# A two-layer hybrid trunk on one core: TensorE in program order through the softmax attention, GLA read-outs of a chunk tile together, and the last gate's products from the last tokens down

## The chip, the core and the metric

The kernel runs on one core of a Trainium2 chip. The metric is the device time of one execution in microseconds; a lower time is better. The engines are named as in the profile: PE is TensorE (PEld its weight loads), DVE is VectorE, ACT is ScalarE, POOL is GpSimd and SP is SyncE, whose queue issues DMAs. Each engine takes its instructions in the order of its own queue and waits on semaphores for the others.

## The reference, cut to what matters

Two layers over 16 meta tokens and 1024 tokens (1040 in all), model width 1024. Each layer projects the normalised input to two head groups: four heads of gated linear attention (GLA), read out from the state at the end of each chunk of 64 tokens and gated by `silu(gr)`, and eight heads of softmax attention with a forgetting bias (FoX). Their normalised outputs go through one output projection; a gated convolutional FFN follows.

```python
def chunk_kv_summary(k, v, log_a):
    log_b = jnp.cumsum(log_a, axis=3)
    log_end = log_b[:, :, :, -1:, :]
    u = jnp.einsum('bhntk,bhntv->bhnkv', k * jnp.exp(log_end - log_b), v)
    return u, jnp.exp(log_end[:, :, :, 0, :])
...
    def step(s, inp):                       # GLA: state at the end of chunk c
        u_c, d_c = inp
        s = d_c[..., None] * s + u_c
        return s, s
    o_r = jnp.einsum('bhntk,bhnkv->bhntv', q_r, states)
...
        logits = (jnp.einsum('bqhd,bkhd->bhqk', q_b, kf)          # FoX
                  + c_b[..., None] - c_k[:, :, None, :])
        logits = jnp.where(key_pos[None, :] <= q_pos[:, None], logits, -jnp.inf)
        return jnp.einsum('bhqk,bkhd->bqhd', jax.nn.softmax(logits, axis=-1), vf)
...
        o_gla = rms_norm(o_gla, gla_norm) * jax.nn.silu(gr)
        h = h + jnp.concatenate([o_gla, rms_norm(o_fox, fox_norm)], axis=-1) @ w_out[i]
        h = h + conv_ffn(rms_norm(h, ffn_norm[i]), w_up[i], conv_w[i], conv_b[i], w_down[i])
```

## The kernel before

**Layout and products.** Activations lie transposed, 128 channels by 1040 tokens a tile. Every dense product is done as three products of split operands (`mm3`, L212 to L218): high times high, low times high, high times low. `unit` (L225) is one tile of 128 output channels over one chunk of tokens, a generator that yields after each of its eight input tiles (seven for the output projection here); `add_tile` (L246) makes one unit for each chunk of tokens. A `Work` list holds such units, and `work.run(us)` issues as many of their steps as fill `us` microseconds by the kernel's own formula; `work.drain()` issues all that is left. So the code itself decides, in its program order, which dense products stand between the pieces of attention.

**Who sets the order on an engine.** The program is written in tiles, and a planner then orders each engine's instructions. It takes them by priority, which is the place in the program, unless a piece is raised with `high_priority(8)` (L800, the scores), and an instruction whose operands the planner does not expect to be ready yet is passed by others. Inside a `manual_schedule` block the named engine keeps program order. The FFN already stands in such a block for PE (L1350); GLA and FoX do not.

**GLA** (`gla_steps`, L474, two passes per layer with two heads each). For each tile group of tokens (16, 384, 384 and 256 of them) PE transposes the keys, `fill(0.5)`; PE makes the increments `u` of all its chunks (L500), `fill(1.0)`; then chunk by chunk DVE makes the next state `St` (L508, from four buffers), PE reads it out for two heads (L513) and `fill(0.3)` follows. Then ACT and DVE normalise the read-outs, `fill(3.0)`, PE transposes them, ACT scales them to `og` and POOL's queue writes them to memory (`ogd`). `fill` issues products of the next head group, the first pass `gla_products` of the second, the second pass `fox_products` of the first FoX head pair.

**FoX** (`fox`, L752). Four head pairs p, two heads e, nine query tiles i (the first of 112 tokens, the others of 116), in groups (7,8), (5,6), (3,4), (1,2), (0), from the last tokens down. One query tile of one head is a slot n; there are 72 slots and 8 more that run out. What a tile needs after its scores is put into later slots: transposes T0, T1, T2 of its probabilities at n+2, the P·V products av0, av1, av2 of its group at n+3, the fold of both heads at n+4, and the store at n+6. A slot issues:

```python
            for kind in ('av0', 'T0'):
                run(n, kind)
...
            parts = [c for c in "12" if (n, "av" + c) in due or (n, "T" + c) in due]
            work.run(fill_us / (1 + len(parts)))
            run(n, "store")
            run(n, "fold")
            for c in parts:
                run(n, "av" + c)
                run(n, "T" + c)
                work.run(fill_us / (1 + len(parts)))
```

with the scores of slot n between the first loop and `parts`. A score tile S is made by two products (L649, L650) in one of three PSUM buffers; DVE adds the bias and takes the running minimum in one pass (L652), ACT takes the exponential to P (L664), which frees S. The transposes of P (L678, L685) go to one of two PSUM buffers `tr`, from which ACT copies the high part (L330) and DVE subtracts the low part (L331) into `PT`. The P·V products (L703) and the fold's transposes `fo` (L716) share one PSUM buffer `av`; ACT and DVE empty the fold (L719, L720). The store's transposes (L742) and the V transposes (L583) use `tr` too.

**What fills FoX.** `plan(-1)` is empty and holds for slots 0 to 3. `plan(0)`, `plan(1)` and `plan(2)` start at slots 4, 22 and 40: three products of the next FoX head pair and one gate (`gr_products`, L601). `plan(3)` at slot 58 is the last gate, h = 3, alone; its result goes to `land[3]` in SBUF (`dst`), while the other gates go through memory. A gate unit's `ev` loads `ogd` on SP's queue (L606) and takes five DVE operations after the first reading of PSUM and three on ACT (L609 to L620). `plan(4)` at slot 62 is the output projection of four tiles of channels, from the last tokens down (chunks of 256, 384 and 400 tokens), input tiles in the order `KORD` = 4, 5, 0, 1, 2, 3, 6. Its operands are split by `split(2)`, `split(1)`, `split(0)` (L944), one for each chunk, the first ahead of everything. Weights are loaded one tile ahead on SP's queue, their high parts made by ACT (L183), their low parts in this stage by POOL (L185).

Of the kernel before, what the change touches and what calls it, by code (L numbers as in the profile page):

```python
# [10 lines left out]
F32 = mybir.dt.float32  # L11
# [13 lines left out]
KD = D // 128  # L25
# [10 lines left out]
CH_FOX = [(0, 344), (344, 348), (692, 348)]  # L36
# [4 lines left out]
M_GK, M_GQ, M_GV, M_GR, M_REM, M_FQ, M_FK, M_FV, M_WO, M_UP = 0, 2, 4, 8, 12, 13, 17, 21, 25, 33  # L41
# [91 lines left out]
class Kern:  # L133
# [213 lines left out]
    def head(self, tiles, pp, nm, feed):  # L347
        s = self.slots
        held, w, waiting = [], [], []
        tags = ("mm", "mm", "S", "S", "S")  # L350
        i = 0
# [97 lines left out]
    def gla_decay(self, lyr, p, gp, pp, g):  # L449
# [4 lines left out]
        for c0, n in CH:  # L454
            z = pp.tile([128, 512], F32, tag="S", name="z")
            nc.tensor.matmul(z[:, :n], self.wau[:, lyr, 128 * p:128 * p + 128], rem[0:16, c0:c0 + n],
# [17 lines left out]
    def gla_steps(self, lyr, p, gp, pp, g, fill):  # L474
        nc = self.nc
        gk, gq, gv, gvm, dec = g["gk"], g["gq"], g["gv"], g["gvm"], g["dec"]
        S = None
        tail = []
        for (c0, n), (t0, t1) in zip([(0, META), (META, 384)] + CH[1:], [(0, 1), (1, 4)] + CTILES[1:]):
            nt = t1 - t0  # L480
            rows = META if t0 == 0 else 128
            kd = gp.tile([128, 3, 128], F32, tag="kd", name="kd", bufs=2)
            tr = pp.tile([128, 4, 128], F32, tag="tr", name="tr")
            for j in range(nt):
                nc.tensor.transpose(tr[:rows, j, :], gk[:, c0 + 128 * j:c0 + 128 * j + rows], self.ident[:])
            nc.vector.tensor_copy(kd[:rows, :nt, :], tr[:rows, :nt, :])
            fill(0.5)
            chunks = [(0, 0, META, None)] if t0 == 0 else \
                [(j, 64 * b, 64 * b + 64, 2 * (t0 - 1 + j) + b) for j in range(nt) for b in range(2)]
            o = [pp.tile([128, 4, 128], F32, tag=("av", "tr")[hh], name="o") for hh in range(2)]  # L490
            us = []
            ub = {}
            for j, r0, r1, c in chunks:
                if r0 not in ub:
                    ub[r0] = pp.tile([128, 4, 128], F32, tag="S", name="u")
                u = ub[r0][:, j, :]
                us.append(u)
                for hh in range(2):
                    val = gvm[:, hh, :] if t0 == 0 else gv[hh][r0:r1, t0 - 1 + j, :]
                    nc.tensor.matmul(u[64 * hh:64 * hh + 64, :], kd[r0:r1, j, 64 * hh:64 * hh + 64], val,  # L500
                                     start=True, stop=True)
            fill(1.0)
            for u, (j, r0, r1, c) in zip(us, chunks):
                Sn = gp.tile([128, 128], F32, tag="St", name="St", bufs=4)
                if c is None:
                    nc.vector.tensor_copy(Sn[:], u)
                else:
                    nc.vector.scalar_tensor_tensor(out=Sn[:], in0=S[:], scalar=dec[:, c:c + 1],  # L508
                                                   in1=u, op0=ALU.mult, op1=ALU.add)
                S = Sn  # L510
                q0 = c0 + 128 * j + r0
                for hh in range(2):
                    nc.tensor.matmul(o[hh][r0:r1, j, :], gq[64 * hh:64 * hh + 64, q0:q0 + r1 - r0],  # L513
                                     S[64 * hh:64 * hh + 64, :], start=True, stop=True)
                fill(0.3)
            ons = []
            for hh in range(2):
                ps = o[hh][:rows, :nt, :]
                sq = gp.tile([128, 3, 128], F32, tag="osq", name="osq")
                nc.scalar.activation(sq[:rows, :nt, :], ps, AF.Square)  # L520
                vv = gp.tile([128, 3], F32, tag="ovv", name="ovv", bufs=2)
                nc.vector.tensor_reduce(out=vv[:rows, :nt], in_=sq[:rows, :nt, :], axis=AX.X, op=ALU.add)
                nc.vector.tensor_scalar(out=vv[:rows, :nt], in0=vv[:rows, :nt], scalar1=1.0 / 128,
                                        scalar2=EPS, op0=ALU.mult, op1=ALU.add)
                y0 = gp.tile([128, 3], F32, tag="oy", name="oy", bufs=2)[:rows, :nt]
                a = gp.tile([128, 3], F32, tag="oa", name="oa", bufs=2)[:rows, :nt]
                self.rsqrt(y0, vv[:rows, :nt], y0, a)
                on = gp.tile([128, 3, 128], F32, tag="on", name="on", bufs=2)
                nc.vector.tensor_tensor(out=on[:rows, :nt, :], in0=ps,
                                        in1=y0.unsqueeze(2).to_broadcast([rows, nt, 128]), op=ALU.mult)  # L530
                ons.append(on)
            fill(3.0)
            for hh in range(2):
                tr = pp.tile([128, 4, 128], F32, tag="tr", name="tr")
                for j in range(nt):
                    nc.tensor.transpose(tr[:, j, :rows], ons[hh][:rows, j, :], self.ident[:rows, :rows])
                og = gp.tile([128, 384], F32, tag="og", name="og", bufs=2)
                nc.scalar.mul(og[:, :n], tr[:].rearrange("p a b -> p (a b)")[:, :n],
                              self.v(lyr, V_GN, 2 * p + hh))
                nc.gpsimd.dma_start(self.ogd[2 * p + hh][:, c0:c0 + n], og[:, :n])  # L540
            fill(0.7)
        self.slots.put(gk, gq, *gv)
# [58 lines left out]
    def gr_products(self, lyr, h, work, ap, pp, nm, dst=None):  # L601
        nc = self.nc

        def ev(ps, c0, n):
            og = ap.tile([128, 348], F32, tag="gog", name="gog", bufs=2)
            nc.sync.dma_start(og[:, :n], self.ogd[h][:, c0:c0 + n])  # L606
            e = ap.tile([128, 348], F32, tag="ge", name="ge", bufs=1)
            x = ap.tile([128, 348], F32, tag="vt", name="gx", bufs=self.vt_bufs)[:, :n]
            nc.vector.tensor_tensor(out=x, in0=ps, in1=nm["r"][:, c0:c0 + n], op=ALU.mult)  # L609
            e, og = e[:, :n], og[:, :n]  # L610
            y = ap.tile([128, 348], F32, tag="gy", name="gy", bufs=1)[:, :n]
            nc.vector.tensor_scalar(out=e, in0=x, scalar1=-87.0, scalar2=None, op0=ALU.max)
            nc.scalar.activation(e, e, AF.Exp, scale=-1.0)
            nc.scalar.activation(y, e, AF.Ln, bias=self.ones[:, 0:1])
            nc.scalar.activation(y, y, AF.Exp, scale=-1.0)
            nc.vector.tensor_tensor(out=og, in0=x, in1=og, op=ALU.mult)
            nc.vector.scalar_tensor_tensor(out=e, in0=e, scalar=1.0, in1=y, op0=ALU.add, op1=ALU.mult)
            nc.vector.scalar_tensor_tensor(out=y, in0=e, scalar=-2.0, in1=y, op0=ALU.add, op1=ALU.mult)
            to = e if dst is None else dst[:, c0:c0 + n]
            nc.vector.scalar_tensor_tensor(out=to, in0=y, scalar=-1.0, in1=og, op0=ALU.mult, op1=ALU.mult)  # L620
            if dst is None:
                nc.gpsimd.dma_start(self.mixd[h][:, c0:c0 + n], e)
        self.add_tile(work, pp, self.wm[lyr, M_GR + h], nm["x"], CH_FOX, ev)


    @staticmethod
# [235 lines left out]
    def attention(self, lyr, nm, hsrc, chunks, feed):  # L862
        tc, nc, s = self.tc, self.nc, self.slots
        with tc.tile_pool(name=f"aps{lyr}", bufs=2, space=PSUM, reuse_waits="tile") as pp2, \
                tc.tile_pool(name=f"aps1{lyr}", bufs=1, space=PSUM, reuse_waits="tile") as pp1, \
                tc.tile_pool(name=f"vm{lyr}", bufs=2, reuse_waits="tile") as self.vmp:
            pp = PsumTags({"mm": (pp2, 2), "S": (pp1, 3), "tr": (pp2, 2), "av": (pp1, 1)})
            qs = [{} for _ in range(4)]
            self.vt_bufs = 3
            with tc.tile_pool(name=f"gla{lyr}", bufs=1, reuse_waits="tile") as gp:  # L870
# [25 lines left out]
                work = Work()  # L896
# [18 lines left out]
            with tc.tile_pool(name=f"att{lyr}", bufs=2, reuse_waits="tile") as ap, \  # L915
                    tc.tile_pool(name=f"lent{lyr}", bufs=1, reuse_waits="tile") as lp:
                s.lent = s.add(lp, 2, f"a{lyr}_")
                box = {}
                KORD = (4, 5, 0, 1, 2, 3, 6)

                def plan(p):
# [33 lines left out]
                            first = {} if m else {"w": ready, "before": {0: lambda: split(1), 1: lambda: split(0)}}  # L955
                            self.add_tile(w, pp, self.wm[lyr, M_WO + m], mix, chunks[::-1], ev, ks=KORD, **first)
                    return w
                self.fox(lyr, ap, pp, qs, plan, lambda: box["mix"][KD - 1])
            for m in range(NSPLIT, KD):
                nc.sync.dma_start(box["hT"][m][:, chunks[0][0]:T], hsrc[m][:, chunks[0][0]:T])  # L960
                s.drop(s.lent)
# [469 lines left out]
```

## Time and profile before

| | us |
|---|---|
| median of 3 runs (lowest, highest) | 2668.52 (2667.55, 2669.83) |
| the profiled execution | 2666.38 |
| its span, first to last instruction | 2664.6 |
| PE busy in the span | 2543.8 (95%) |
| mean granted TensorE clock | 0.988 |

The stages of the first layer, in microseconds from the span's start: GLA with its products up to about 193, FoX to 556 (with four tiles of the output projection), the rest of the output projection and the FFN's start to 700, the FFN after that. The second layer's FoX runs from 1510 to 1877.

In the lines of the profile, `out<-in` names the tile that an instruction writes and those it reads; Lnnn is the line of the kernel. In a view of waits the columns are the total idle time, how often, and the longest. In a timeline they are the start, the duration, the engine and what it does, and in brackets the idle time before and who ended it. PE's matmuls are pipelined: one may start before the last is shown as ended.

### The profile page before, as it was taken

Reading aid. Unit: us, or ns where it says so; the run is one execution under the profiler, and the core shown is the slowest. Engines: PE = TensorE matmul, PEld = TensorE weight load, DVE = VectorE, ACT = ScalarE, POOL = GpSimd, SP = SyncE. Lnnn points to the kernel's source line nnn. Section 1 sums busy time; section 2 is a strip of 40 time slices with the busy share of each in tenths; the row PEclk is TensorE's granted clock in tenths of the full one; section 3 lists DMA queues with packets and bytes.
Section 4 is the critical chain, followed back from the end, with each engine's and each line's share of the span. In section 5 each row is a group of like instructions: output and inputs, shape, how many; then the busy total and the mean of one; then the engine's idle time right before and its main releaser. Section 6 shows DMA issues by size and latency. Waiting matters only on the chain.

```text
span 2664.6 us, 46352 instructions
## 1 busy us (share of the span) xinstructions
PE 2543.8 (95%) x18102; PEld 2408.9 (90%) x18102; DVE 1760.6 (66%) x3484; ACT 1240.2 (47%) x2677; POOL 458.1 (17%) x596
## 2 busy tenths in 40 slices
PE   8999999897999999999999999998979999999997
PEld 7888888897999999999998788888979999998886
DVE  7555666759867777643665566666698777776335
ACT  6336665535545445421443455665455444453112
POOL 4023333333000000000200333333320000000002
PEclk9999999998999999999999999999989999999999
DMA  3132133341222222631312222243412222245212
GB/s 124 57 90 52 55 87 114 115 130 62 96 81 76 84 77 91 216 93 57 105 52 64 70 75 60 69 123 100 146 59 90 77 82 80 72 139 197 66 55 76
DMA packets 114476, 240.72 MB, mean 90 GB/s; under 512 B 14432, under 2 KB 36192, under 8 KB 114256
## 3 DMA queue, kind: packets, MB, share of 16 engines
q1 hardware_dynamic: 96000, 182.27, 22.3%
q0 software_dynamic: 16384, 53.18, 5.4%
q8 instruction: 142, 2.33, 0.4%
q10 hardware_dynamic: 1872, 2.31, 0.2%
q14 instruction: 78, 0.64, 0.1%
HBM read 174.01 MB, written 50.91 MB: 84 GB/s over the span
## 4 chain that ended last, share of the span: by engine, by line
PE 62%; issue 18%; DVE 12%; ACT 4%; DMA 2%; POOL 2%; SPq 0%; DVEq 0%; POOLq 0%; ACTq 0%
PE mm L216 12%; PE mm L218 11%; PE mm L217 11%; PE up L216 5%; PE up L218 5%; PE up L217 5%; PE av L703 2%; PE tr L685 2%; DVE S L652 1%; DVE x L1035 1%; PE wo L217 1%; PE wo L216 1%; PE wo L218 1%; DMA cb<-cd 1%; DVE PT L331 1%
## 5 line engine op out<-in xcount | busy, mean ns | idle before, releaser
L216 PE MATMUL up<-x,hi 128*128 128x260 f32 (+1 forms) x2464 | 700.0, 284 | 22.8 <-DVE hu L1177 20.3
L217 PE MATMUL up<-x,lo 128*128 128x260 f32 (+1 forms) x2464 | 698.1, 283 | 0.0
L218 PE MATMUL up<-x,hi 128*128 128x260 f32 (+1 forms) x2464 | 697.4, 283 | 0.0
L216 PEld LDWEIGHTS up<-x,hi 128*128 128x128 f32 x2464 | 466.6, 189 | 24.3 <-DVE hu L1177 20.7
L217 PEld LDWEIGHTS up<-x,lo 128*128 128x128 f32 x2464 | 466.9, 190 | 0.1
L218 PEld LDWEIGHTS up<-x,hi 128*128 128x128 f32 x2464 | 466.9, 189 | 0.0
L216 PE MATMUL mm<-xh,hi 128*128 128x348 f32 (+4 forms) x1056 | 369.8, 350 | 0.0
L218 PE MATMUL mm<-xl,hi 128*128 128x348 f32 (+4 forms) x1056 | 340.8, 323 | 0.0
L217 PE MATMUL mm<-xh,lo 128*128 128x348 f32 (+4 forms) x1056 | 340.4, 322 | 0.0
L1011 DVE TENSOR_TENSOR lo<-raw,hi 128x512 fp32r<-128x512 f32 x308 | 213.4, 695 | 144.4 <-ACT hi L1010 144.4
L183 ACT CAST hi<-raw 128x512 fp32r<-128x512 f32 (+1 forms) x264 | 142.4, 543 | 339.6 <-PE mm L218 249.2
L217 PE MATMUL mm<-ah,lo 128*128 128x400 f32 (+1 forms) x760 | 266.1, 350 | 1.7 <-DVE lo L185 1.7
L216 PE MATMUL mm<-ah,hi 128*128 128x400 f32 (+1 forms) x760 | 265.6, 349 | 0.0
L218 PE MATMUL mm<-al,hi 128*128 128x400 f32 (+1 forms) x760 | 265.6, 349 | 0.0
L185 DVE TENSOR_TENSOR lo<-raw,hi 128x512 fp32r<-128x512 f32 (+1 forms) x196 | 120.8, 620 | 182.6 <-ACT hi L183 179.1
L1010 ACT CAST hi<-raw 128x512 fp32r<-128x512 f32 x308 | 190.2, 620 | 105.7 <-PE up L218 92.2
L216 PEld LDWEIGHTS mm<-xh,hi 128*128 128x128 f32 x1056 | 200.4, 190 | 14.3 <-issue 13.5
L217 PEld LDWEIGHTS mm<-xh,lo 128*128 128x128 f32 x1056 | 200.7, 190 | 0.5 <-issue 0.3
L218 PEld LDWEIGHTS mm<-xl,hi 128*128 128x128 f32 x1056 | 199.6, 189 | 0.3 <-issue 0.3
L1200 POOL DMA_DIRECT2D actd<-cv x44 | 23.4, 533 | 831.1 <-DVE cv L1199 831.1
L331 DVE TENSOR_TENSOR PT<-tr,PT 116x464 fp32r<-116x464 f32 (+3 forms) x240 | 122.3, 516 | 61.4 <-ACT PT L330 59.7
L664 ACT ACTIVATE P<-S,m 116x460 f32<-116x460 f32 (+2 forms) x224 | 125.0, 562 | 79.9 <-DVE m L652 76.5
(248 smaller groups left out, 5287.0 us busy)
## 6 DMA issues: line engine op xcount, KB each, us to landing
raw<-in_wm_dram SPq DMA_DIRECT2D x328, 256.0 KB, 2.6
raw<-in_wd_dram SPq DMA_DIRECT2D x64, 256.0 KB, 2.6
actd<-cv POOLq DMA_DIRECT2D x22, 520.0 KB, 3.0
st<-actd SPq DMA_DIRECT2D x22, 520.0 KB, 4.5
actd<-cv POOLq DMA_DIRECT2D x22, 512.0 KB, 3.0
st<-actd SPq DMA_DIRECT2D x22, 512.0 KB, 4.1
cb<-cd SPq DMA_DIRECT2D x16, 520.0 KB, 4.4
kA<-kA SPq DMA_DIRECT2D x24, 260.0 KB, 3.9
```

The source lines that it names most:

```text
L183: nc.scalar.copy(hi[:, :n, :], raw[:, :n, :])
L185: eng.tensor_tensor(out=lo[:, :n, :], in0=raw[:, :n, :], in1=hi[:, :n, :].bitcast(F32), op=ALU.subtract)
L216: nc.tensor.matmul(ps, wh, xh[:, c0:c0 + n], start=first, stop=False, skip_group_check=more)
L217: nc.tensor.matmul(ps, wl, xh[:, c0:c0 + n], start=False, stop=False, skip_group_check=more)
L218: nc.tensor.matmul(ps, wh, xl[:, c0:c0 + n], start=False, stop=last, skip_group_check=more)
L331: nc.vector.tensor_tensor(out=lo, in0=src, in1=hi.bitcast(F32), op=ALU.subtract)
L652: nc.vector.tensor_tensor_reduce(out=S[:rows, :n], in0=S[:rows, :n], in1=cb[:rows, c0:k1], scale=1.0, scalar=(BIG if ci == 0 else m[:rows, ...
L664: nc.scalar.activation(P[:rows, :n], S[:rows, :n], AF.Exp, scale=-1.0, bias=m[:rows, nch - 1:nch], accum_out=(den if nch == 1 else d3[:row ...
L685: nc.tensor.transpose(tr[:w, j, :rows], P[:rows, o:o + w], id_)
L703: nc.tensor.matmul(av[:, a:width], w.rearrange("p a b -> p (a b)"), x, start=(t == 0 and i == 0), stop=(t == last and i == 1))
L1010: nc.scalar.copy(hi[:], src[:])
L1011: nc.vector.tensor_tensor(out=lo[:], in0=src[:], in1=hi[:].bitcast(F32), op=ALU.subtract)
```

## The change

Three edits. In `gla_steps` all states of a tile group are made first (eight `St` buffers in place of four), then one fill of 0.3 for each chunk together, and then the read-outs of all its chunks. In `gr_products` the last gate, the one with a `dst`, takes its three chunks of tokens from the last to the first. And `fox` is called inside a `manual_schedule` block for PE, so that PE keeps program order through FoX.

```diff
@@ gla_steps
             fill(1.0)
+            Ss = []
             for u, (j, r0, r1, c) in zip(us, chunks):
-                Sn = gp.tile([128, 128], F32, tag="St", name="St", bufs=4)
+                Sn = gp.tile([128, 128], F32, tag="St", name="St", bufs=8)
                 if c is None:
                     nc.vector.tensor_copy(Sn[:], u)
                 else:
                     nc.vector.scalar_tensor_tensor(out=Sn[:], in0=S[:], scalar=dec[:, c:c + 1],
                                                    in1=u, op0=ALU.mult, op1=ALU.add)
                 S = Sn
+                Ss.append(Sn)
+            fill(0.3 * len(chunks))
+            for Sn, (j, r0, r1, c) in zip(Ss, chunks):
                 q0 = c0 + 128 * j + r0
                 for hh in range(2):
                     nc.tensor.matmul(o[hh][r0:r1, j, :], gq[64 * hh:64 * hh + 64, q0:q0 + r1 - r0],
-                                     S[64 * hh:64 * hh + 64, :], start=True, stop=True)
-                fill(0.3)
+                                     Sn[64 * hh:64 * hh + 64, :], start=True, stop=True)
@@ gr_products
-        self.add_tile(work, pp, self.wm[lyr, M_GR + h], nm["x"], CH_FOX, ev)
+        self.add_tile(work, pp, self.wm[lyr, M_GR + h], nm["x"], CH_FOX if dst is None else CH_FOX[::-1], ev)
@@ attention
-                self.fox(lyr, ap, pp, qs, plan, lambda: box["mix"][KD - 1])
+                with tc.manual_schedule(engines={mybir.EngineType.PE}):
+                    self.fox(lyr, ap, pp, qs, plan, lambda: box["mix"][KD - 1])
```

## The prediction

> **What bounds the kernel now.** I read busy time by stage first (per stretch: PE, weight loads, VectorE, ScalarE, GpSimd, then granted clock, DMA share, GB/s), then TensorE's (PE's) waits inside the stages that change, and last the timeline where those waits are.
>
> ```profile
> span 2664.6 us, 46352 instructions
> ...
> 0.00:193.00 193.00, 180.94 (x1225) 155.48 (x1225) 121.18 (x271) 87.68 (x205) 47.07 (x62) 0.99 0.27 88
> 193.00:556.00 363.00, 334.95 (x2310) 316.22 (x2309) 239.81 (x743) 216.43 (x647) 122.73 (x175) 0.99 0.29 85
> ...
> 1510.00:1877.00 367.00, 337.94 (x2312) 319.27 (x2312) 240.24 (x744) 216.40 (x647) 122.69 (x175) 0.98 0.28 84
> ```
>
> PE is the bound: VectorE (DVE) is busy 240 us of a FoX stretch, PE 335 of 363. It idles 28.1 and 29.1 us in the two stretches, and these 57 us, with what half clock costs there, are all that a better order can win. Who ended the idle times (first stretch, then second):
>
> ```profile
> PE tr L685 <- DVE PT L331: 9.4, 9, 2.1
> PE av L703 <- DVE ff L720: 5.2, 8, 1.2
> PE tr L678 <- DVE PT L331: 4.8, 4, 1.9
> PE mm L216 <- ACT mh L330: 4.4, 1, 4.4
> PE mm L217 <- POOL lo L185: 2.0, 3, 1.0
> PE tr L742 <- DVE PT L331: 1.4, 3, 0.7
> ...
> PE tr L685 <- DVE PT L331: 8.5, 9, 1.2
> PE tr L678 <- DVE PT L331: 6.8, 4, 3.5
> PE av L703 <- DVE ff L720: 5.1, 8, 1.2
> PE mm L216 <- ACT mh L330: 4.4, 1, 4.4
> ```
>
> Transposes wait for a PSUM buffer that DVE still reads, 32.3 us in all (9.4+4.8+1.4+8.5+6.8+1.4); the first P·V product after a fold waits for the fold's PSUM bank, 10.3 us; and the output projection waits 4.4 us per layer for one operand.
>
> **Part 1, program order in FoX: the start (+16 us).** The slots n of `fox` take filling products only from slot 4 on: `plan(-1)` is empty. Today the planner lays products of `plan(0)` between the first scores. In program order PE runs scores, transposes and one P·V alone, and all of it hangs on DVE's score pass and ScalarE's (ACT's) exponentials through three S buffers. The timeline shows that chain as it runs today:
>
> ```profile
> 194.46 0.49 PE L583 MATMUL tr<-ident,vt 128*116 128x128 f32 x3
> 196.63 0.64 DVE L652 CUSTOM_DVE_ANT_0 S<-S,cb 116x460 f32<-116x460 f32 x1
> 198.60 0.65 ACT L664 ACTIVATE P<-S,m 116x460 f32<-116x460 f32 x1 [1.64 <-DVE m L652]
> 199.68 0.37 PE L649 MATMUL S<-kA,qA 128*116 128x460 f32 x1
> 201.03 0.86 PE L685 MATMUL tr<-ident,P 116*116 116x116 f32 x7
> 208.64 0.64 ACT L664 ACTIVATE P<-S,m 116x460 f32<-116x460 f32 x1 [0.76 <-DVE m L652]
> 209.09 1.05 PE L703 MATMUL av<-PT,V 112*128 112x232 f32 x7 [0.22 <-DVE PT L331]
> 210.01 0.40 PE L649 MATMUL S<-kA,qA 128*116 128x348 f32 x1
> ...
> 194.95:209.50 14.55, 14.24 (x90) 12.63 (x89) 9.98 (x33) 9.46 (x30) 4.11 (x7) 1.00 0.17 59
> ```
>
> The exponentials of slot 3 begin at 208.64; they free the buffer of slot 4's second score tile, which runs at 210.01. Without products in front it could run some 0.6 us earlier, so filling starts at about 209.5. From 194.95 (the last V transpose) that is 14.5 us. PE's own work in it: nine pairs of score products, at most 0.42 us a pair (3.4; one takes 0.37, a part of which overlaps the next), 21 transposes at 0.09 (1.9; seven start within 0.63), eight P·V at 0.13 (1.0): 6.3 us. So 8.2 us idle against 0.3 now (last row: 14.24 of 14.55): +8 per layer. Bounds: +5, if DVE takes the first scores 2 us earlier and the chain shortens by one; +13, if PE also runs at half clock there.
>
> That clock is seen in the second layer: granted clock by windows (the column before the last two):
>
> ```profile
> 1611.42:1614.40 2.98, 0.99 (x6) 0.98 (x7) 2.12 (x6) 2.65 (x9) 0.00 (x0) 1.00 0.00 0
> 1614.40:1617.80 3.40, 3.40 (x15) 3.27 (x14) 2.36 (x7) 1.03 (x3) 0.99 (x2) 0.50 0.32 105
> 1700.00:1703.10 3.10, 0.01 (x1) 0.00 (x0) 1.85 (x8) 2.79 (x7) 0.55 (x1) 1.00 0.00 1
> 1703.10:1706.50 3.40, 2.94 (x11) 2.77 (x11) 2.36 (x7) 1.20 (x5) 0.56 (x1) 0.50 0.28 87
> ```
>
> Three microseconds with PE a third busy, or not at all, were followed by 3.4 us at 0.50. The start would be 43% busy (6.3 of 14.5), above the first of these, so I charge no half clock to it. The Trainium skill ("TensorE: Matmul & The Clock Gate", "What's actually happening") says that the clock halves after an idle window of about 3.4 us and is whole again after a busy one. These rows agree on the length, but a window that was a third busy sufficed. By that rule the start, with pauses of 2 to 3 us only, stays whole and the sum is +8; by the first row a window a little emptier than its mean would be halved, and the sum is that of the rival on the clock, +14. The two half-clock windows shown cost half of their 6.3 busy us; the waits ahead of them (2.0 and 3.5 us, both transposes) are of the kind that the new order spreads: −3 us.
>
> **Part 1, folds (+13 us).** In a slot the order is av0, T0, scores, fill, store, fold, then av1/T1 with fill only if there are such parts. For the tile groups (5,6), (3,4) and (1,2) the fold's slot has none, so the fold's transposes are followed at once by the next slot's av0, which needs the same single `av` bank. For the groups (7,8) and (0) a fill of nine products and some transposes lies between, some 1.7 us. The shortest fold today:
>
> ```profile
> 260.87 0.60 PE L716 MATMUL fo<-ident,avs 128*116 128x128 f32 x4
> 261.50 0.37 ACT L719 COPY ff<-fo 116x256 f32<-116x256 f32 x1
> 261.91 0.42 DVE L720 TENSOR_TENSOR ff<-fo,ff 116x256 f32<-116x256 f32 x1
> 262.39 0.71 PE L703 MATMUL av<-PT,V 112*128 112x232 f32 x4
> ```
>
> From 261.47 to 262.39 are 0.92 us, now hidden by scores, transposes and products. Bare, it is 3 folds × 4 head pairs × 2 layers × 0.97 (0.92 and a little queue) = 23.3, less the 10.3 of now: +13. Behind the waiting av0 stand T0 and the scores of its slot, so DVE and ACT get those as much later; they have two slots of slack. Bounds: +12 at 0.92; +28 if every third one is like today's longest such wait, 1.2 us behind a fill of 1.7, 2.9 bare (16 × 0.92 + 8 × 2.9 = 38).
>
> **Part 1, transposes (−6 us).** With two `tr` buffers a transpose group waits for the evacuation two groups back:
>
> ```profile
> L330 ACT CAST PT<-tr 116x464 fp32r<-116x464 f32 x64 | 34.7, 546 | 26.5 <-PE tr L685 26.0
> L331 DVE TENSOR_TENSOR PT<-tr,PT 116x464 fp32r<-116x464 f32 x64 | 40.6, 637 | 10.5 <-ACT PT L330 10.2
> 279.00:300.00 21.00, 18.46 (x129) 17.16 (x130) 19.24 (x59) 15.14 (x44) 6.75 (x10) 1.00 0.26 83
> ```
>
> Free, that is 0.55+0.64 us and hand-overs, about 1.35; behind two exponentials of 0.65 it is some 2.6. The tightest place in program order has two fills of six products (0.157 us apart) and little else between, 2.1 us: enough for tiles 0 to 6, half a microsecond short for 7 and 8, where two slots a head pair meet it. At the seam of two head pairs DVE is full (19.24 of 21 us, third row: the gate's evacuation with the longest scores) and PE idles 2.5 there now; I leave that. 2.5 + 0.8 = 3.3 for each of eight head pairs is 26 of 32.3. Bounds: 12 (the short tiles' excess alone and half of the seam) and 41 (0.5 us at two more slots of each).
>
> **Part 2, the last gate reversed (−12 us).** The first unit of the output projection takes the last 256 tokens; its sixth operand is the gated head, whose last tokens are now evacuated last:
>
> ```profile
> 479.71 0.52 DVE L620 SCALAR_TENSOR_TENSOR h<-gy,gog 128x344 f32<-128x344 f32 x1
> 491.06 0.51 DVE L609 TENSOR_TENSOR gx<-mm,r 128x348 f32<-128x348 f32 x1
> 498.03 0.51 DVE L620 SCALAR_TENSOR_TENSOR h<-gy,gog 128x348 f32<-128x348 f32 x1
> 498.99 1.82 DVE L331 TENSOR_TENSOR ml<-h,mh 128x384 fp32r<-128x384 f32 x4
> 499.06 0.58 PE L216 MATMUL mm<-mh,hi 128*128 128x256 f32 x1 [4.41 <-ACT mh L330]
> 498.20:505.03 6.83, 5.89 (x21) 5.29 (x22) 6.29 (x16) 3.86 (x12) 2.56 (x5) 0.50 0.58 184
> ```
>
> Reversed, that chunk is done where the first one is today, at about 480. The wait of 4.41 goes, and with it half of the 5.89 busy us at clock 0.50: 7.3 per layer. No instruction, DMA or byte is added: three `ogd` loads change places on SP's queue. Next late is the split of the middle 384 tokens (498.99 to 500.8): I leave 1.3 us. 2 × (7.3 − 1.3) = 12. Bounds: 15 and 4, for a middle split as late as the first. The waits for `lo` from POOL (2.0 per layer) I leave: no buffer of theirs changes; 2 less to 4 more.
>
> **Part 3, GLA read-outs together (0).** The same read-outs, with one run of PE behind the last state in place of one behind each, and four more state buffers. They move behind the fill that was spread between them, so the evacuation behind a group keeps `fill(3.0)` as cover and loses one `fill(0.3)`. The planner still orders PE here, and the 12 us that PE idles in the first 193 (first stage row) hold the kernel's own start too. Without that cover each of the four passes would end 0.3 × 1.6 = 0.5 us later; −1 to +2.
>
> **Sum.** 16 + 13 − 6 − 12 − 3 = +8 us on the profiled execution's 2666.4 (span 2664.6, 1.8 around it), hence 2674.4 for a run like it; it stands 2.1 below the median of 2668.5, so I forecast 2676.5. What measurement can tell here is about 0.2%, 5.3 us. The forecast's own range is 2670 to 2682.
>
> **Rivals.**
> - *The cover suffices* (28%): transposes wait 12 us only, the start costs 10, folds +12, the gate gives 15, the clock 3: −16, 2652.5. For it: 13 transpose waits per stretch are few for 72 slots, and even slots smooth the bursts on DVE. Against: the start and the bare folds are fixed by code.
> - *VectorE becomes the bound at the seams* (18%): where slots cannot lend each other products, each of six seams (279 to 300 is one) costs 2 us more and the transposes keep their 32: 8 + 12 + 6 = +26, 2694.5. It decides where PE's own work in a seam falls 2 us or more under DVE's 19.24; today PE did 18.46 there with products borrowed from later. Against: the gate's evacuation can run late unseen.
> - *The clock* (12%): the start runs at 0.50, 3 us more per layer (one window of 3.4 us into the fill and slower scores): +14, 2682.5.
> - *The order hardly changes* (12%): within 0.2%, 2668.5. Against: PE is full from 194.95 to 209.50 today, with 8 us of products that no slot before 4 has.
>
> The forecast has 30%. Faster is the first rival, 0.28; within 0.2% is the last and a fifth of the forecast, 0.18; slower the rest, 0.54. Range 2648 to 2702: the ends are the first rival with 4 us more and the seams with 8 us more.
>
> **What would show it.** Right: PE idle between 195 and 210 with scores, transposes and no `mm`; `av L703 <- DVE ff L720` near 11 us per stretch instead of 5.2; no wait on `mh` above 2 us and no 0.50 behind it. Wrong: FoX stretches under 355 us, or a start filled with `mm` after all; wrong the other way: transposes waiting above 20 us per stretch.

## The result, and the profile after

| | before | after |
|---|---|---|
| time, us (range) | 2668.5 (2667.55 to 2669.83) | 2694.14 (2691.86 to 2698.1) |
| ratio to before, 95% interval | | 1.0095 (1.0083 to 1.0108) |
| profiled execution, its span | 2666.38, 2664.6 | 2692.89, 2691.1 |
| mean granted TensorE clock | 0.988 | 0.977 |

The change costs 25.6 us; 8 were forecast. In the profile of the changed kernel the lines of the code are 3 or 4 higher than before (fold L719, its addition L723, P·V L706, transposes L681 and L688, scores L652, read-outs L517). First the two FoX stretches, by windows (PE, weight loads, VectorE, ScalarE, GpSimd, granted clock, DMA share, GB/s):

```profile
span 2691.1 us, 46410 instructions
...
181.00:571.00 390.00, 341.49 (x2313) 323.77 (x2312) 239.73 (x751) 218.62 (x649) 122.89 (x176) 0.96 0.26 79
1513.00:1902.00 389.00, 344.31 (x2314) 326.57 (x2313) 239.34 (x751) 218.86 (x649) 123.53 (x176) 0.95 0.26 79
```

FoX is now 390 and 389 us long against 363 and 367. PE idles 48.5 and 44.7 us in it against 28.1 and 29.1: 36 more. VectorE's work is the same 240 us, so VectorE has not become the bound of the stretch. But two columns say more than idle time: PE's busy time rose by 6 to 7 us a stretch with no instruction added, and the clock fell from 0.99 and 0.98 to 0.96 and 0.95. And the first stretch starts at 181 instead of 193: the stage ahead of it became 12 us shorter.

Who ended PE's idle times in the first stretch, then in the second:

```profile
PE av L706 <- DVE ff L723: 18.9, 16, 4.1
PE tr L681 <- DVE PT L331: 12.9, 4, 4.8
PE S L652 <- ACT P L667: 5.2, 2, 5.0
PE tr L688 <- DVE PT L331: 4.4, 5, 1.6
PE mm L217 <- POOL lo L185: 3.3, 3, 1.4
PE tr L539 <- DVE on L532: 1.8, 1, 1.8
PE tr L745 <- DVE PT L331: 1.0, 4, 0.2
...
PE av L706 <- DVE ff L723: 19.2, 16, 4.1
PE tr L681 <- DVE PT L331: 8.5, 4, 2.9
PE S L652 <- ACT P L667: 5.2, 2, 5.0
PE tr L688 <- DVE PT L331: 4.5, 5, 1.6
PE mm L217 <- POOL lo L185: 3.3, 3, 1.4
```

The fold's wait (av on ff) grew from 10.3 to 38.1 us over both layers. The wait on `mh` is gone. The transposes wait 32.3 us, as before to a tenth, but not in the same place: those in mid-pair (L688) fell from 17.9 to 8.9, those of the longest tile at the seams (L681) rose from 11.6 to 21.4.

**Half clock.** The half-clock windows of the two stretches after the change, eleven; those at the two starts, and the sum of all:

```profile
187.50:194.30 6.80, 3.60 (x11) 2.51 (x12) 3.97 (x13) 2.74 (x10) 0.84 (x2) 0.50 0.02 4
197.70:201.10 3.40, 3.40 (x13) 2.96 (x14) 2.16 (x7) 2.02 (x7) 0.20 (x1) 0.50 0.00 0
...
1518.70:1535.80 17.10, 11.98 (x44) 9.70 (x45) 10.21 (x33) 8.73 (x27) 2.81 (x6) 0.50 0.05 16
...
sum 64.70, PE 49.69 PEld 45.02 DVE 41.31 ACT 34.99 POOL 12.54; mean PE 4.52 PEld 4.09 DVE 3.76 ACT 3.18 POOL 1.14
```

and the four windows before:

```profile
sum 20.40, PE 18.26 PEld 16.75 DVE 17.23 ACT 9.90 POOL 6.69; mean PE 4.57 PEld 4.19 DVE 4.31 ACT 2.48 POOL 1.67
```

Work done at half clock takes twice as long: two score products of 464 columns start 0.39 us apart at 191.42, at clock 0.50, and 0.20 apart at 181.47, at the whole clock. So half of the busy time is the price: 9.1 us before, 24.8 after, +15.7. Half of 3.60, 3.40 and 11.98, that is 9.5 us, is lost at the starts; the other eight windows stand behind the six seams and behind the longest fold wait of each layer.

**The read-outs.** The gain is in GLA, where PE hardly idled. The groups of instructions between 70 and 193 us, before (busy time and mean ns of one):

```profile
L513 PE MATMUL o<-St,gq 64*64 64x128 f32 x128 | 13.1, 295 | 0.0
L500 PE MATMUL u<-gv,kd 64*64 64x128 f32 x128 | 4.9, 279 | 0.0
```

and after:

```profile
L517 PE MATMUL o<-St,gq 64*64 64x128 f32 x128 | 4.9, 279 | 0.0
```

The same 128 products of the same shape took 13.1 us in small runs and 4.9 in large ones, as the increments `u` always did. The row counts the time in which at least one such product is in flight, so each run also adds the tail of its last product (one is shown as some 0.28 us long). What a run costs is read from the starts in the timeline; before:

```profile
112.77 0.44 PE L513 MATMUL o<-St,gq 64*64 64x128 f32 x4
113.14 0.45 PE L216 MATMUL mm<-xh,hi 128*128 128x400 f32 x1
...
113.87 0.43 PE L513 MATMUL o<-St,gq 64*64 64x128 f32 x4
```

and after:

```profile
112.42 0.89 PE L517 MATMUL o<-St,gq 64*64 64x128 f32 x24
113.23 0.44 PE L216 MATMUL mm<-xh,hi 128*128 128x384 f32 x1
```

Four read-outs and three products repeat every 1.10 us. The three products take 0.18 each where they follow one another, so one chunk's read-outs cost 0.56: 0.37 from the first read-out to the next product, and 0.19 by which the products on both sides are late. A run of 24 (six chunks) takes 0.81 and the same 0.19. None of this is a wait in the trace; it counts as busy time.

From the first read-out to the first score the stage took 114.9 us in each layer before (78.03 to 192.94, 1395.09 to 1510.04), and takes 102.3 and 102.0 after (78.67 to 180.97, 1411.03 to 1513.07): −25.5 us.

So the 26.5 us by which the span grew are +36 of idle time in FoX, +15.7 of half clock, −25.5 in GLA: +26.

**Where a stall went.** The fold of the last head pair's longest group (the last 232 tokens), around 500 us:

```profile
497.10 0.60 PE L719 MATMUL fo<-ident,avs 128*116 128x128 f32 x4
...
498.23 1.22 ACT L330 CAST mh<-h 128x384 fp32r<-128x384 f32 x3
...
500.60 1.58 DVE L623 SCALAR_TENSOR_TENSOR h<-gy,gog 128x348 f32<-128x348 f32 x1
...
500.94 0.37 ACT L722 COPY ff<-fo 116x256 f32<-116x256 f32 x1
...
502.10 0.88 DVE L331 TENSOR_TENSOR ml<-h,mh 128x256 fp32r<-128x256 f32 x2
...
502.97 0.41 DVE L723 TENSOR_TENSOR ff<-fo,ff 116x256 f32<-116x256 f32 x1
...
503.44 2.06 PE L706 MATMUL av<-PT,V 112*128 112x232 f32 x8 [4.11 <-DVE ff L723]
```

The fold is ready at 497.7. ScalarE then casts `mh`, and besides it runs the gate's last exponential, the high part of a weight tile and the exponentials of two score tiles; the fold's copy waits its turn until 500.94. VectorE finishes the gate and the low parts `ml`, and the fold's addition waits until 502.97. The work for which PE used to wait at `mh` is now a good part of what stands in front of the fold, and half clock follows here (501.5 to 508.3) as it did there.

**A seam.** VectorE at the first seam, ahead of the wait of 4.82:

```profile
292.60 0.34 DVE L615 TENSOR_SCALAR ge<-gx 128x348 f32<-128x348 f32 x1 [1.78 <-DMA mixd<-ge]
...
293.99 0.53 ACT L330 CAST PT<-tr 116x464 fp32r<-116x464 f32 x1
...
294.94 0.52 DVE L620 SCALAR_TENSOR_TENSOR ge<-ge,gy 128x348 f32<-128x348 f32 x1 [0.99 <-ACT gy L618]
...
296.31 0.64 DVE L331 TENSOR_TENSOR PT<-tr,PT 116x464 fp32r<-116x464 f32 x1
...
297.10 0.42 PE L681 MATMUL tr<-ident,Ps 116*116 116x116 f32 x1 [4.82 <-DVE PT L331]
```

VectorE is not full here. It stands 1.78 us in front of a gate operation whose one buffer `ge` is still being stored, and 0.99 in front of another that waits for ScalarE's exponential; behind both stands the subtraction that would free `tr`. The store is not there at every seam: VectorE waits 1.8 and 2.4 us for it at the first and the third, where PE waits 4.82 and 4.24, and not at the second, where PE still waits 3.11. No run gave `ge` a second buffer. By windows, in the 16 us around it, after:

```profile
284.00:300.00 16.00, 10.82 (x72) 10.29 (x70) 10.93 (x29) 7.95 (x24) 5.23 (x7) 0.90 0.31 86
```

and around the same seam before:

```profile
280.00:296.00 16.00, 13.79 (x96) 12.76 (x95) 14.43 (x46) 12.25 (x36) 5.21 (x7) 1.00 0.26 85
```

VectorE did 14.43 us of work in that time before and 10.93 after.

### The profile page after: what moved, and what is told of

Read it like the earlier page. It is cut to its first block, busy times and chain, and to the rows that moved or that the text cites. A ratio compares the mean times of both kernels' runs of the same rounds, so it can differ in the third digit from the quotient of the medians.

```text
span 2691.1 us, 46410 instructions
## 1 busy us (share of the span) xinstructions
PE 2537.1 (94%) x18102; PEld 2424.5 (90%) x18102; DVE 1755.4 (65%) x3484; ACT 1243.0 (46%) x2677; POOL 457.6 (17%) x596
## 4 chain that ended last, share of the span: by engine, by line
PE 60%; issue 20%; DVE 13%; ACT 4%; POOL 2%; DMA 1%; DVEq 0%; SPq 0%; POOLq 0%; ACTq 0%
PE mm L216 11%; PE mm L217 11%; PE mm L218 11%; PE up L216 5%; PE up L218 5%; PE up L217 5%; PE av L706 2%; DVE S L655 2%; PE tr L688 2%; DVE x L1039 1%; PE wo L217 1%; PE wo L216 1%; PE wo L218 1%; PE S L652 1%; PE S L653 1%
## 5 line engine op out<-in xcount | busy, mean ns | idle before, releaser
L216 PE MATMUL up<-x,hi 128*128 128x260 f32 (+1 forms) x2464 | 701.3, 285 | 22.4 <-DVE hu L1181 20.3
L216 PE MATMUL mm<-xh,hi 128*128 128x348 f32 (+4 forms) x1056 | 360.9, 342 | 0.0
```

Source lines behind the costliest of these rows:

```text
L216: nc.tensor.matmul(ps, wh, xh[:, c0:c0 + n], start=first, stop=False, skip_group_check=more)
```

## The experiments

All times are medians; the kernel before ran beside each group (2666.4, 2667.0 and 2666.2 us), and ratios are to it. Beside the whole change it stood at 2668.5, so a difference in microseconds between runs of different groups is good to about 2 us.

### One part at a time

Program order alone, on the kernel before:

```diff
-                self.fox(lyr, ap, pp, qs, plan, lambda: box["mix"][KD - 1])
+                with tc.manual_schedule(engines={mybir.EngineType.PE}):
+                    self.fox(lyr, ap, pp, qs, plan, lambda: box["mix"][KD - 1])
```

> The kernel before with program order on TensorE in the softmax attention and nothing else of the change. Theory A (program order alone loses: unfilled starts, bare folds, seams with half clock behind them; the reversed gate gains nothing in it): 2690 to 2698 us, like the whole change. Theory B (order loses more and the reversed gate gives back about 12 us as forecast): 2702 to 2708 us. Rival C (a good part of the loss is of the reversed gate or of the grouped read-outs): below 2686 us.

2710.82 us, 1.0173 (1.0152 to 1.0194): +44.5, more than any of the three had. So something in the whole change gives back 17 us.

The reversed gate alone, on the kernel before:

```diff
-        self.add_tile(work, pp, self.wm[lyr, M_GR + h], nm["x"], CH_FOX, ev)
+        self.add_tile(work, pp, self.wm[lyr, M_GR + h], nm["x"], CH_FOX if dst is None else CH_FOX[::-1], ev)
```

> The kernel before with the reversed order of the last gate alone, TensorE still laid out by the planner. Theory A and B: the wait of 4.41 us on mh and the half clock behind it go in both layers, 2655 to 2662 us. Rival C (the reversal costs by its evacuations or DMAs): 2668 us or more; then a new wait of the output projection or of a fold shows near the place of the old one.

2666.97 us, 1.0001 (0.9991 to 1.0010): nothing. The waits of its first FoX stretch:

```profile
PE tr L685 <- DVE PT L331: 11.1, 11, 2.0
PE tr L678 <- DVE PT L331: 8.0, 4, 2.9
...
PE tr L742 <- DVE PT L331: 2.1, 4, 0.8
```

The wait on `mh` is gone, as forecast. The transposes wait 21.2 us here against 15.6, 5.6 more than before, and in the second stretch 19.4 against 16.7. The stall was removed and its time was not.

The change without program order (reversed gate and grouped read-outs, PE laid out by the planner):

```diff
-                with tc.manual_schedule(engines={mybir.EngineType.PE}):
-                    self.fox(lyr, ap, pp, qs, plan, lambda: box["mix"][KD - 1])
+                self.fox(lyr, ap, pp, qs, plan, lambda: box["mix"][KD - 1])
```

> The change without program order: reversed gate and grouped GLA read-outs under the planner. All theories hold the grouping at -1 to +2 us, so within 3 us of the run with the gate alone. If it is 5 us or more above that one, the grouping costs what I held at nothing.

2644.17 us, 0.9921 (0.9904 to 0.9937). That is 23 us under the run with the gate alone, where I had expected at most 3: the grouping is worth what I held at nothing. It also shows what program order costs beside the rest: 2694.1 − 2644.2 = 50 us, or 48 if each is taken against the kernel before beside it.

The change without the reversed gate (`CH_FOX` for all gates):

```diff
-        ... CH_FOX if dst is None else CH_FOX[::-1], ev)
+        ... CH_FOX, ev)
```

> The change without the reversed gate: program order and grouped read-outs. Theory A: within 4 us of the whole change (2690 to 2698 us), the mh wait is back and the fold wait of 4.1 us at its side gone. Theory B: 2702 to 2708 us. Rival C: below 2690 us.

2693.79 us, 1.0106 (1.0087 to 1.0125): as the whole change. The wait on `mh` was back, but only 1.9 us a layer, and the fold's longest wait is 3.5 without the reversal too. Under program order there was hardly a stall left for the reversal to remove, and theory A's claim that the reversal had made the fold's wait falls.

The grouped read-outs alone, on the kernel before (the first hunk of the change):

> The kernel before with the grouped GLA read-outs alone. Theory A (the grouping is worth about 23 us by the fewer runs of read-outs, the reversed gate nothing): 2641 to 2648 us, as with both (2644). Rival (grouping and reversed gate help each other: the reversed gate gains its wait once the rest is shorter): 2650 us or more.

2652.14 us, 0.9954 (0.9941 to 0.9966). The grouping alone gains 14 us, and the reversed gate, worth nothing alone, takes 8 off beside it, which is the rival's number. But the traces show that the gate gains nothing of its own there either. In microseconds of the profiled executions, the first layer and then the second, all under the planner:

| | before | gate alone | read-outs alone | both |
|---|---|---|---|---|
| first read-out to first score | 114.9, 114.9 | 114.9, 114.9 | 102.3, 103.6 | 102.3, 102.1 |
| first score to last fold | 355.6, 359.3 | 360.8, 355.9 | 361.0, 365.0 | 359.8, 357.0 |
| idle time of PE in the second row | 27.3, 28.3 | 28.3, 26.5 | 28.8, 29.2 | 27.3, 26.0 |
| price of half clock in it | 3.0, 6.2 | 7.6, 4.3 | 6.4, 10.5 | 6.7, 4.7 |

The grouping's gain in GLA is 24 to 25 us with and without the gate. FoX is 2 us longer than before with the gate, whether the read-outs are grouped or not, and 11 us longer with the grouped read-outs alone; 8 of these 11 are half clock. So the 14 us are 24 less what FoX lost. Why the planner's order of FoX gets more half clock in that one kernel stays open.

### The size of a run of read-outs

The change without program order, and read-outs in runs of two chunks:

```diff
-            fill(0.3 * len(chunks))
-            for Sn, (j, r0, r1, c) in zip(Ss, chunks):
+            for i, (Sn, (j, r0, r1, c)) in enumerate(zip(Ss, chunks)):
+                if i % 2 == 0:
+                    fill(0.6)
```

> The change without program order, but with the GLA read-outs in runs of two chunks with a fill ahead of each, instead of one run for a pass (a pass has six chunks). Theory A (each run of read-outs between products costs some 0.3 us of its own beside 0.14 us a chunk, so a run per chunk costs 0.57 us each): three runs a pass in place of one, 2 passes of six and some rests per head pair, gives back about half of the 23 us: 2652 to 2657 us, and the read-out row about 280 ns wide only inside the runs, 7 to 9 us in all against 4.9 and 13.1. Rival (the gain of grouping is not in TensorE's runs but in the later evacuation or in the planner's laying out of the rest): within 4 us of 2644, or all of it lost, 2664 or more, with the read-out row not in step with the time.

2657.74 us, 0.9966 (0.9954 to 0.9979), 0.7 us above the range of theory A, between the 2667.0 of single chunks and the 2644.2 of whole passes. The row between 70 and 190 us:

```profile
L518 PE MATMUL o<-St,gq 64*64 64x128 f32 x128 | 7.2, 295 | 0.0
```

7.2 us lie between 13.1 and 4.9. The lengths of the runs in the first layer, from the first read-out to the next product, as means from the traces:

```
read-outs in a run     4      8      16     24
us                   0.36   0.38   0.60   0.82
runs: before          30      2
      pairs            2     16
      whole passes     2             2      4
```

Eight read-outs cost hardly more than four. The price is that of a run, 0.37 and the 0.19 around it, up to about eight read-outs. 32 runs, 18 and 8 runs so cost 18, 10 and 6.6 us a layer. That predicts gains of 8 and 11 us a layer; the stage became 6.1 and 7.2 us shorter with pairs (two layers), 12.6 and 12.9 with whole passes. With pairs the stage also has one window of half clock a layer, at 108.3 and at 1408.8, which costs 1.7 us and which neither of the others has. The Trainium skill ("TensorEngine Tiling (Array Packing)", "Key Properties") says that a change of the tiling mode drains TensorE. The read-outs use 64 of the array's rows, the products around them 128, and a price by the run and not by the read-out agrees with it; no run here tells a drain from another cost of changing over.

### What program order loses

Products from slot 0, in the whole change:

```diff
-        starts = [f + 4 for f in first] + [first[3] + 8, len(steps) + 8]
+        starts = [0] + [f + 4 for f in first[1:]] + [first[3] + 8, len(steps) + 8]
```

> The whole change, with the products of plan(0) handed out from slot 0 instead of slot 4. Theory A (the unfilled start costs idle time and half clock): the wait of 5.0 us of S on P and the half-clock windows at 187.5 to 201.1 and 1518.7 to 1535.7 go, 8 to 16 us less than the change: 2678 to 2686 us. Rival (the start waits on the gated chain of ScalarE and VectorE, which products in front do not shorten, and the products taken there are missing later): 2690 to 2696 us.

2689.11 us, 1.0081 (1.0063 to 1.0100): 5 us better than the change, with an interval that overlaps the change's own, and between the two ranges, nearer to the rival's. The wait of S on P fell only from 5.0 to 3.0, and the first half-clock windows of the stretches shrank from 10.2 and 17.1 us to 3.4 each, but new waits came: S on a transfer of kL (2.6), as the first pair's keys are now needed sooner after their copies, and transposes in mid-pair up to 2.5. The start does cost idle time and half clock, yet most of that is the chain through VectorE and ScalarE, which products in front do not shorten. In the whole change this chain begins ahead of the scores: PE makes the first score at 180.97, but VectorE's first score pass runs at 187.75, behind the evacuations of V that ScalarE and VectorE hand to and fro from 183.58 to 187.84.

Store and fold ahead of the fill, where a slot has no later parts, in the whole change:

```diff
+            if not parts:
+                run(n, "store")
+                run(n, "fold")
             work.run(fill_us / (1 + len(parts)))
             run(n, "store")
             run(n, "fold")
```

> The whole change, with store and fold ahead of the filling products in the slots that have no later parts. Theory A (24 folds wait bare for 0.92 us and a little): the wait of av on ff falls from 38 us in both layers to 10 to 16, the time by 15 to 25 us: 2669 to 2679 us. Rival (the wait moves to the transposes or the scores, since VectorE's and ScalarE's work stays where it is): 2685 us or more, with waits of tr on PT grown by what ff loses.

2671.2 us, 1.0012 (1.0003 to 1.0022): 23 us better than the change. Waits of its two stretches:

```profile
PE av L706 <- DVE ff L723: 10.5, 7, 3.5
...
PE av L706 <- DVE ff L723: 9.8, 7, 3.6
```

The fold's wait fell from 38.1 to 20.3 us, somewhat above the 10 to 16 that theory A had; what is left is the long one at the last pair and smaller ones at the seams. The transposes wait as before (L681 and L688 together 17.4 in the first stretch against 17.3), so nothing moved there. Theory A holds, but for the size of what is left.

The transposes' evacuation ahead of the gate's, in the whole change:

```diff
-                self.fox_transposes(i, ci, P, PT, FT * ti, pp)
+                with self.tc.high_priority(8):
+                    self.fox_transposes(i, ci, P, PT, FT * ti, pp)
```

> The whole change, with the evacuation of the transposes put ahead of the gate's in the planner's order on VectorE and ScalarE (the same raised priority that the scores have). Theory A (at the seams the transposes wait because the planner puts the gate's evacuation in front of PT, not because VectorE is full): waits of tr on PT at the six seams fall from 21.4 us to under 8, half clock behind them goes, 10 to 25 us less: 2669 to 2684 us. Rival (VectorE is full at the seams): same time within 5 us, the wait turns up as S or ff.

2704.94 us, 1.0142 (1.0121 to 1.0163): 11 us worse. Both theories fall. The first stretch:

```profile
PE tr L688 <- DVE PT L331: 10.9, 10, 2.1
PE tr L681 <- DVE PT L331: 5.8, 3, 2.5
```

The seams' waits halved (21.4 to 11.5 over both layers), which VectorE could not have done were it full. But the transposes in mid-pair wait 21.8 instead of 8.9, and both starts have 17.1 us at half clock.

The run with the fold ahead, and the evacuation of the other gates cut to one operation and the store. The other eight operations of each unit (five on VectorE, three on ScalarE; the expectation counts ten) and the load of `ogd` are left out, so this kernel no longer computes the gate:

```diff
+            if dst is None:
+                e = ap.tile([128, 348], F32, tag="ge", name="ge", bufs=1)[:, :n]
+                nc.vector.tensor_tensor(out=e, in0=ps, in1=nm["r"][:, c0:c0 + n], op=ALU.mult)
+                nc.gpsimd.dma_start(self.mixd[h][:, c0:c0 + n], e)
+                return
```

> As the run with the fold ahead of the fill (2671.2 us), but the evacuation of the gate's products of heads 0 to 2 is one product with r on VectorE and a store; the ten other operations and the load of each of these nine units per layer are left out. Theory A (the seams stall because the gate's chain of VectorE and ScalarE operations stands in front of the transposes' evacuations in two in-order queues): the waits of tr L681 at the six seams (18 us of the 21.9) fall below 8 and the half clock behind them goes: 2645 to 2656 us. Rival (the seams stall by the longest scores and their transposes alone): 2662 us or more, the waits on Ps still 2 to 4 us each.

2635.55 us, 36 less than with it, more than theory A had. Of the seams' transposes (L686 in this kernel) one wait a stretch is left, 0.4 us in the first and 0.8 in the second, from which these rows are:

```profile
PE tr L693 <- DVE PT L331: 9.3, 9, 1.6
...
PE av L711 <- DVE ff L728: 4.1, 1, 4.1
...
PE tr L686 <- DVE PT L331: 0.8, 1, 0.8
```

No half-clock window stands behind a seam; those at the starts and at the last fold remain. So the seams stall by the gate's evacuation, not by the longest scores. The 36 us are an upper bound for the seams' price, since the kernel also has less to do elsewhere: the smaller fold waits went too (the fold's wait is the one of 4.1 alone).

### Two combinations

Both repairs of the order of issue, in the whole change (the hunks of the start and of the fold together):

> The whole change with both repairs of issue order: products from slot 0, fold ahead of the fill. Theory A (the two are in different places and add up: -23 and -5): 2664 to 2668 us, as long as before and 20 us above the change without program order. Rival (the products taken at the start are missing as cover in the first pair's folds or seam): 2671 us or more.

2669.54 us, 1.0009 (0.9999 to 1.0018), between the two ranges. It is 1.7 us below the run with the fold alone, and the two intervals overlap, so no gain of the start beside the fold is shown. Program order with both repairs is as long as before, although it has the grouping's gain.

The change without program order, and with the fold ahead of the fill:

> The change without program order and with store and fold ahead of the fill. Theory A (bare folds are the price of program order; the planner already covers folds, whose waits are 4.0 us a stretch): 2638 to 2648 us. Rival (the order of issue sets the planner's priorities too, and the fold wait falls with it): 2636 us or less.

2636.11 us, 0.9889 (0.9875 to 0.9902). This beats both kernels, before by 30 us and after by 58. It is 8 below the run without program order, at the upper end of the rival's range; but the fold's wait hardly fell:

```profile
PE tr L688 <- DVE PT L331: 5.1, 6, 2.0
PE tr L681 <- DVE PT L331: 4.7, 3, 1.8
PE av L706 <- DVE ff L723: 3.4, 5, 1.0
```

The gain is in the transposes (L688: 12.3 without the edit, 5.1 here). Neither theory had that. A likely reason is that the place in the program is the planner's priority, so that an earlier fold changes what it puts beside the transposes; no run shows it.

## Why the prediction was right and wrong

The sign was right, and the time lies in the wide range, but outside the forecast's own 2670 to 2682. That the wide range held was luck: two large terms were missed, and they are of opposite sign. The forecast's terms against the profile of after, both layers together, in us:

| term | forecast | measured | from |
|---|---|---|---|
| read-outs together | 0 | −25.5 | first read-out to first score |
| start, idle | +16 | +10.4 | S on P, 5.2 twice |
| folds | +13 | +27.8 | av on ff, 10.3 to 38.1 |
| transposes with the seams | −6 | 0 | 32.3 both times |
| wait on mh | −6.2 | −8.8 | 4.4 to none, twice |
| wait on lo | 0 | +2.6 | 2.0 to 3.3, twice |
| other waits | | +4.1 | rest of the 36.1 of idle time |
| half clock | −8.8 | +15.7 | half of the work in such windows |
| sum | +8 | +26.3 | span: +26.5 |

(Of the forecast's −12 for the gate, 5.8 were half clock; they stand with the −3 in the last row but one.)

**Read-outs, "0".** The step that failed is "The same read-outs, with one run of PE behind the last state": I priced the waits that the new order makes and took the products' own time as fixed. The view of groups of the kernel before held the hint, 13.1 us against 4.9 for equal rows; I read the stage's 180.94 of 193 as work that had to be done. The runs of one part, of pairs and of whole passes show the price.

**Half clock, "I charge no half clock to it".** I took the fuller of the two windows seen, a third busy, as a threshold. The windows ahead of the starts' half clock show how far that holds:

```profile
184.10:187.50 3.40, 1.04 (x9) 0.66 (x7) 1.16 (x4) 1.87 (x7) 1.10 (x2) 0.99 0.77 249
194.30:197.70 3.40, 2.25 (x14) 1.37 (x14) 2.88 (x10) 2.39 (x8) 0.43 (x1) 1.00 0.00 0
```

The second was two thirds busy and half clock followed. The Trainium skill ("TensorE: Matmul & The Clock Gate", "What's actually happening") speaks of an idle window; here the measurement decides, and windows partly busy sufficed. PE's busy time in this profile gives no threshold, though: the window from 1607.40 to 1610.80 was busy for 1.88 us, less than that second one, and the clock stayed whole behind it. I also let the clock gain 3 us because the old transposes' waits would spread; they did not spread, they gathered at the seams. The rival on the clock was right about the starts, with 6 us for the 9.5 lost there; no case had charged half clock to the seams.

**Folds, "+13".** The bare folds were right: a layer has nine waits of 0.92 us, as worked out, and three of 1.5 to 1.7, so 26 us in both against the 23.3 forecast, and the run with the fold ahead takes 23 us off. The cover that I granted to the groups (7,8) and (0) was not enough: two waits of 4.1 and six smaller ones stand there; at the long ones it was not the fill that was short, but the queues of ScalarE and VectorE that were long, as the timeline of the fold shows.

**Transposes, "−6".** The estimate for mid-pair was right in direction (17.9 to 8.9). "PE idles 2.5 there now; I leave that" failed: the seams went from 11.6 to 21.4, and each has half clock behind it.

**The rival "VectorE becomes the bound at the seams"** had 2694.5, and the time is 2694.1. This is no confirmation. Its place is right and its condition is not: VectorE did less in the seam than before, and a mere change of its order halved the seam's waits. The seams cost because two queues in order, VectorE's and ScalarE's, hand the gate's chain to and fro in front of the transposes; and its sum holds no −25 for the read-outs.

**The reversed gate, "−12".** The wait went as forecast. The gain came through nowhere: under the planner FoX is 2 us longer with the reversal than before, both alone and beside the grouped read-outs, and the 8 us that it takes off beside the grouped read-outs are a loss that FoX had with the grouping alone. Alone, the transposes took the time (8.3 us more in both layers against the 8.8 of `mh`); in program order the wait was 1.1 to 1.9 us already, since the same work stood in front of the fold.

**Program order** as a whole costs 44 to 50 us, against the +20 that its terms without the gate summed to (16 + 13 − 6 − 3).

## What to carry to other kernels

Compare rows of equal shape and count in the groups of the kernel before: where one takes more than twice as long, the products' surroundings can cost, and not their work, which no view of waits shows; then read the starts in the timeline, since the row counts each run's tail too. When an order is fixed by hand on one engine, read it slot by slot for the piece whose consumer comes next, and put that piece ahead of the filling work. A stall that was taken away here brought nothing while the work that caused it stayed; look for where the same instructions of the other queues stand next.

## What the runs showed of the hardware

A run of 64-row products between 128-row products costs 0.56 us whether it has four or eight of them. Half clock followed a window of 3.4 us in which PE was busy 2.25, and did not follow another with 1.88, and at the second start it went on for 17.1 us with PE busy 70% (11.98 of 17.10). Eleven windows of half clock cost 25 us, as much as the grouping gained.
